# Hymba layer: half of w_out split ahead into DRAM, and the first SSD group's gating moved into the second group

## The chip, the cores and the metric

The kernel runs on one NeuronCore of a Trainium2 chip. The metric is the device time of one execution in microseconds (us). The engines go by the profile's names: PE (TensorE, matmuls), PEld (its weight loads), DVE (VectorE), ACT (ScalarE), POOL (GpSimd) and SP (SyncE, which here only issues DMAs). DMAs are issued on the queues of SP, of POOL and, in the changed kernel, of ACT.

## The reference

One layer over 1024 tokens of width 1024, in float32. All products run on one input projection, whose columns feed a bidirectional state-space branch (SSD, 16 heads in 2 groups, chunks of 128 tokens) and a windowed attention branch (16 heads, 4 KV heads, window 128). Each is gated with SiLU and normed; both go through one output projection.

```python
h = rms_norm(x, norm_in_g)
z, xbc, dt_raw, q, k, v, ga = jnp.split(h @ w_in, PROJ_SPLITS, axis=-1)
xs, Bm, Cm = split(silu(conv5(xbc) + conv_b))            # depthwise, 5 taps
y = ssd(xs, dt_f, ...) + rev(ssd(rev(xs), rev(dt_b), ...)) + d_skip * xs
y_ssd = rms_norm(y * silu(z), ssd_norm_g)                # per group of 512
o = windowed_gqa(q, k, v, rel_bias, sink)                # |i-j| <= 128
y_attn = rms_norm(o * silu(ga), attn_norm_g)
out = x + concat([y_ssd, y_attn]) @ w_out                # w_out: 2048 x 1024
return rms_norm(out, final_norm_g)
```

## The kernel before

Every large product is computed as three PE passes over a high and a low part (hi x hi, hi x lo, lo x hi, type fp32r). So each weight must be split before use: load, an ACT copy that rounds to the high part, and a subtraction that leaves the low part. The input projection runs over 38 weight blocks of 1024 x 128, each loaded once (wraw), split (whi, wlo; the subtraction goes to POOL for every third block, else to DVE) and multiplied with the two halves of the tokens, which stay in SBUF as hhi and hlo.

The stages, by the time of the profile: start (norm, first blocks, the dt and v block), to 58 us; convolutions and backward SSD loop of group 0, to 184; its forward loop, to 297; convolutions of group 1, to 380; its backward loop, to 450; its forward loop, to 540; attention, to about 790; last output products and final norm, to 900. In the SSD stages PE has little SSD work of its own. The function fill(n) puts n halves of projection blocks (24 matmuls of 128 x 512 each) into the loops, and the table FORWARD says how many go where in a forward loop.

In the backward loop, chunks 7 to 0, each chunk's state contribution yo is added to yb_d in DRAM by an accumulating POOL DMA (yb_d already holds the skip term d_skip * xs, written after the convolutions). In the forward loop the chunk's yb starts as the forward state's contribution; an accumulating POOL DMA at line 716 adds yb_d to it in SBUF (chunk 0 is loaded plainly by SP), and at line 723 DVE adds the product y of the scores with the inputs. Then the chunk is gated (lines 726 to 735): zt is loaded, POOL multiplies yb by zt into yg (L729), SP stores yg to y_d, ACT squares (L732), POOL adds the squares in two steps (L733, L735), and after four chunks PE sums them (L605).

w_out's 2048 rows are 16 blocks kb of two pieces of 128 x 512, so 32 "chores". In a chore SP loads a piece (oraw), ACT scales it by the norm's gain (L519) and copies it into hhi (L520), POOL subtracts into hlo (L521): w_out's halves take the place of the projection's hhi and hlo once these are read for the last time. The chores stand between the steps of the attention.

The attention has 32 steps (KV head by query block): logits on PE, a DVE operation with bias and row minimum (L966), the exponential on ACT (L969), transposes on PE (L977), their split on ACT and DVE (L982, L983), products with v. Between them, up to 20 matmuls of projection or output products are fed to PE per step.

The order on each engine is made by a scheduler that lists instructions by a simulated timeline; each engine then works strictly in that order. tc.issue_after(x) keeps an instruction behind x on its queue. A tile of a pool with bufs=1 is one buffer: the next tile of that name waits until every reader of the last one, a DMA too, is done.

Of the kernel before, what the change touches and what calls it, by code (L numbers as in the profile page):

```python
# [10 lines left out]
F32 = mybir.dt.float32  # L11
# [24 lines left out]
def kernel(  # L36
# [21 lines left out]
    def scratch(name, shape, dt):  # L58
        if dbg is not None and name in dbg:
            return dbg[name]  # L60
        return tc.dram_tile(shape, dt, name=name)
# [10 lines left out]
    yb_d = scratch("yb_d", [NG, NSB, P, 512], F32)  # L72
    y_d = scratch("y_d", [NG, NSB, P, 512], F32)
    rd_d = scratch("rd_d", [NKV, 2, 2, 16, 64], F32)
    o_d = scratch("o_d", [NSB, 2, P, 512], F32)

    def pool(stack, name, bufs=1, **kw):
# [182 lines left out]
    def pad_tile():  # L260
# [2 lines left out]
        G.memset(pad[:, S + 2:S + 4], 0.0)  # L263
        return pad

    pads = {}
    square(0)
    root(0)
# [44 lines left out]
    wlo = s1.tile([P, NKB, 288], F32R, tag="wvlo", name="wvlo")  # L313
    wvraw = s1.tile([P, NKB, 288], F32, tag="wvraw", name="wvraw")
    nc.sync.dma_start(out=wvraw, in_=w_vdt)
    ordered(lambda: A.activation(out=whi, in_=wvraw, func=AF.Copy))
    ordered(lambda: G.tensor_tensor(out=wlo, in0=wvraw, in1=whi.bitcast(F32), op=ALU.subtract))
    with tc.issue_after(line["EngineType.Pool"].ins):
        both, dtb, Ab, rb, dsk, msk = small_tables()

    for t, src in zip((snk, dsk), both):
        for a in range(2):
# [177 lines left out]

    def fetch():
        n = split[0] + len(raws)
        if n < len(chores) and len(raws) < RB:
            kb, c = chores[n]
            raw = yp.tile([P, 512], F32, tag="oraw", name="oraw", bufs=RB)
            nc.sync.dma_start(out=raw, in_=w_out[kb * P:(kb + 1) * P, c:c + 512])
            raws.append(raw)

    def chore():
        if split[0] < allowed[0]:  # L510
            if not raws:
                fetch()
            kb, c = chores[split[0]]
            split[0] += 1
            raw = raws.pop(0)
            i, j = divmod(kb % 8, 4)
            hi, lo = (t[i][:, 2 * j:2 * j + 2, :].rearrange("p b e -> p (b e)") for t in (hhi, hlo))
            gain = prm_sb[:, 80 + kb:81 + kb]
            A.activation(out=raw, in_=raw, func=AF.Copy, scale=gain)  # L519
            A.activation(out=hi[:, c:c + 512], in_=raw, func=AF.Copy)  # L520
            G.tensor_tensor(out=lo[:, c:c + 512], in0=raw, in1=hi[:, c:c + 512].bitcast(F32), op=ALU.subtract)  # L521
            wout[kb] = hi, lo
            for _ in range(RB):
                fetch()

    def chores_up_to(n):
        while split[0] < n:
# [69 lines left out]

    sums = []

    def add_sums():  # L600
        ps = bank("t")
        todo = sums[:4]
        del sums[:4]
        for i, (g, c, t) in enumerate(todo):
            T.matmul(ps[:, i:i + 1], lhsT=t, rhs=ones[:, 0:1], start=True, stop=True)  # L605
        g, c, t = todo[0]
        V.tensor_copy(ssq[:, g, c:c + 4], ps[:, 0:4])

    for g in range(NG):
# [4 lines left out]
        for b in range(4):  # L614
            cv = cp.tile([P, S], F32, tag="acc", name="cv")
            th = conv(4 * g + b, cv)
            A.activation(out=th, in_=cv, func=AF.Copy, scale=dsk[:, 4 * g + b:4 * g + b + 1])
            nc.sync.dma_start(out=yb_d[g, :, :, b * P:(b + 1) * P].rearrange("c p l -> p c l"),
                              in_=th.rearrange("p (c l) -> p c l", c=NSB))
            to_tokens(cv, xk[:, :, b * P:(b + 1) * P])  # L620

        if g == NG - 1:
            cpc.close()
# [24 lines left out]
        def y_off(Sx, c, d, dst):  # L648
            et = sp.tile([P, 4, P], F32, tag="et", name="et")
            r = es_d[d, c * NH + g * HPG:c * NH + g * HPG + 1, :]  # L650
            for a in range(2):
                nc.sync.dma_start(out=et[a * 64:(a + 1) * 64].rearrange("p b l -> p (b l)"),
                                  in_=bass.AP(tensor=r.tensor, offset=r.offset + a * 4 * P, ap=[[0, 64], [1, 4 * P]]))
            ps = bank("s")
            for b in range(4):
                T.matmul(ps[:, b * P:(b + 1) * P], lhsT=Sx[:, b * P:(b + 1) * P],  # L656
                         rhs=CT[:, c * P:(c + 1) * P], start=True, stop=True)
            V.tensor_tensor(out=dst, in0=ps, in1=et.rearrange("p b l -> p (b l)"), op=ALU.mult)

        Sb = None  # L660
        for c in range(NSB - 1, -1, -1):
            if Sb is not None:
                yo = sp.tile([P, 512], F32, tag="yo", name="yo", bufs=3)
                y_off(Sb, c, 1, yo)
                G.dma_start(out=yb_d[g, c], in_=yo, accum_op=ALU.add)
            if c > 0:
                Sb = advance(Sb, c, 1)
            if c == 5 and sums:
                add_sums()
            fill(1)  # L670
        Sf = None
# [35 lines left out]
        for c in range(NSB):  # L707
            M = Mn
            if c < NSB - 1:
                Mn = scores(c + 1)  # L710
            yb = sp.tile([P, 512], F32, tag="yo", name="yb", bufs=3)
            if Sf is None:
                nc.sync.dma_start(out=yb, in_=yb_d[g, c])
            else:
                y_off(Sf, c, 0, yb)
                G.dma_start(out=yb, in_=yb_d[g, c], accum_op=ALU.add)
            fill(FORWARD[c][0])
            py = bank("y")
            for h in range(HPG):
                a = h % 2 * 64  # L720
                T.matmul(py[a:a + 64, h // 2 * P:(h // 2 + 1) * P], lhsT=xk[:, c, h * 64:(h + 1) * 64],
                         rhs=M[:, h, :], start=True, stop=True)
            V.tensor_tensor(out=yb, in0=py, in1=yb, op=ALU.add)
            if c < NSB - 1:
                Sf = advance(Sf, c, 0)
            zt = sp.tile([P, 4, P], F32, tag="zt", name="zt", bufs=1)
            nc.sync.dma_start(out=zt, in_=z_d[g * 4:(g + 1) * 4, :, c * P:(c + 1) * P].rearrange("b p s -> p b s"))
            yg = sp.tile([P, 512], F32, tag="yg", name="yg", bufs=1)
            G.tensor_tensor(out=yg, in0=yb, in1=zt.rearrange("p b s -> p (b s)"), op=ALU.mult)  # L729
            nc.sync.dma_start(out=y_d[g, c], in_=yg)  # L730
            y2 = sp.tile([P, 512], F32, tag="y2", name="y2", bufs=1)
            A.activation(out=y2, in_=yg, func=AF.Square)  # L732
            G.tensor_tensor(out=y2[:, 0:256], in0=y2[:, 0:256], in1=y2[:, 256:512], op=ALU.add)  # L733
            sqs = sp.tile([P, P], F32, tag="sqs", name="sqs", bufs=6)
            G.tensor_tensor(out=sqs, in0=y2[:, 0:P], in1=y2[:, P:256], op=ALU.add)  # L735
            sums.append((g, c, sqs))
            if c == 5:
                add_sums()
            if g == NG - 1 and c == 4:
                load_kv(0, 0)  # L740
                load_q(0, 0)
                load_q(0, 1)
            fill(FORWARD[c][1])
# [403 lines left out]
```

## Time and profile before

| | us |
|---|---|
| median of 3 runs | 902.15 (900.38 to 902.24) |
| profiled execution | 901.8 |
| its span | 900.0 |
| PE busy in the span | 850.9 (95%) |
| DVE busy | 574.5 (64%) |
| ACT busy | 488.1 (54%) |
| POOL busy | 366.9 (41%) |

The profile shows one execution. Times count from the span's start; an engine's busy time counts its instructions, not its DMA issues or waits. "Granted clock" is the share of TensorE's full clock that the chip gave it in a stretch. The rows further below come from the same execution; a row's bracket, as [2.41 <-DVE yb L723], says how long the engine had stood idle before that instruction and what ended the wait.

### The profile page before, as it was taken

What the parts mean: (1) busy time and instruction counts of PE and PEld (TensorE: products, weight loads), DVE (VectorE), ACT (ScalarE), POOL (GpSimd) and SP (SyncE); (2) the same over time, 40 slices, a digit from 0 to 9 for tenths busy, and PEclk for the clock granted to TensorE, in tenths of its full rate; (3) what the DMA queues carried; (4) which work ended last, traced back from release to release, by engine and by line L of the source; (5) the groups of instructions that cost most, each with busy time, mean ns of one, the idle gap of its engine ahead of it and who ended that gap; (6) DMA issues with size and microseconds to landing.
All of it is one profiled execution on the core that took longest, in us unless ns stands there. A gap on an engine that the chain in (4) does not pass through costs nothing.

```text
span 900.0 us, 13343 instructions
## 1 busy us (share of the span) xinstructions
PE 850.9 (95%) x4622; PEld 716.0 (80%) x4622; DVE 574.5 (64%) x975; ACT 488.1 (54%) x1112; POOL 366.9 (41%) x331
## 2 busy tenths in 40 slices
PE   6999999998999999999969999999999999799997
PEld 5998788886777888888847787887888888688786
DVE  5675665696897476447769935655766667556433
ACT  5622573464565345524645626788767866765222
POOL 4331012534764201244257551274553741735622
PEclk9999999999999999999998999999999999999999
DMA  9042563675888413577859869879755757424421
GB/s 354 8 114 65 178 192 119 174 220 166 234 233 254 133 47 94 153 189 195 225 145 264 218 182 263 228 197 326 224 152 174 216 132 186 141 59 133 133 87 47
DMA packets 127408, 154.25 MB, mean 171 GB/s; under 512 B 42331, under 2 KB 79899, under 8 KB 127212
## 3 DMA queue, kind: packets, MB, share of 16 engines
q1 hardware_dynamic: 121420, 141.35, 51.7%
q0 software_dynamic: 5776, 11.79, 7.5%
q8 instruction: 36, 0.59, 0.3%
q14 instruction: 32, 0.26, 0.1%
q10 hardware_dynamic: 144, 0.26, 0.1%
HBM read 111.58 MB, written 43.88 MB: 173 GB/s over the span
## 4 chain that ended last, share of the span: by engine, by line
PE 58%; DMA 15%; DVE 10%; issue 7%; POOL 5%; ACT 3%; SPq 1%; POOLq 0%; DVEq 0%; ACTq 0%
PE mm L154 30%; PE mm L781 13%; PE y L999 3%; DMA cb<-cs_d 3%; DMA oraw<-in_w_out_dram 3%; PE s L963 3%; DMA yb<-yb_d 2%; DMA rdb<-rd_d 2%; DMA et<-es_d 2%; PE mm L372 2%; PE t L977 2%; DMA yb_d<-yo 1%; PE s L656 1%; DVE M L702 1%; DMA zt<-z_d 1%
## 5 line engine op out<-in xcount | busy, mean ns | idle before, releaser
L154 PE MATMUL mm<-hlo,whi 128*128 128x512 f32 (+1 forms) x640 | 247.4, 387 | 0.9 <-DVE rs L243 0.5
L154 PE MATMUL mm<-hhi,whi 128*128 128x512 f32 (+1 forms) x640 | 247.9, 387 | 0.0
L154 PE MATMUL mm<-hhi,wlo 128*128 128x512 f32 (+1 forms) x640 | 247.2, 386 | 0.0
L154 PEld LDWEIGHTS mm<-hlo,whi 128*128 128x128 f32 x640 | 121.7, 190 | 24.5 <-issue 1.7
L154 PEld LDWEIGHTS mm<-hhi,wlo 128*128 128x128 f32 x640 | 122.0, 191 | 22.0 <-issue 0.7
L154 PEld LDWEIGHTS mm<-hhi,whi 128*128 128x128 f32 x640 | 122.1, 191 | 21.5 <-issue 0.5
L781 PE MATMUL mm<-hhi,yl 128*128 128x512 f32 (+1 forms) x264 | 104.8, 397 | 0.7 <-POOL yl L773 0.7
L781 PE MATMUL mm<-hhi,yh 128*128 128x512 f32 (+1 forms) x264 | 104.7, 397 | 0.0
L781 PE MATMUL mm<-hlo,yh 128*128 128x512 f32 (+1 forms) x264 | 104.6, 396 | 0.0
L966 DVE CUSTOM_DVE_ANT_0 lg<-s,bias,nsnk 128x320 f32<-128x320 f32 (+2 forms) x128 | 64.5, 521 | 42.3 <-PE s L963 41.4
L969 ACT ACTIVATE lg<-lg,nm 128x320 f32<-128x320 f32 (+2 forms) x128 | 68.5, 535 | 18.5 <-DVE nm L966 16.6
L336 DVE SCALAR_TENSOR_TENSOR acc<-pad,prm_sb,acc 128x1024 f32<-128x1024 f32 x48 | 62.1, 1300 | 23.4 <-ACT acc L333 22.1
L773 POOL TENSOR_TENSOR yl<-y,yh 128x512 fp32r<-128x512 f32 x32 | 41.9, 1309 | 83.8 <-ACT yh L772 59.1
L145 POOL TENSOR_TENSOR wlo<-wraw,whi 128x1024 fp32r<-128x1024 f32 x12 | 30.1, 2509 | 71.0 <-ACT whi L142 71.0
L142 ACT ACTIVATE whi<-wraw 128x1024 fp32r<-128x1024 f32 x36 | 37.9, 1053 | 38.2 <-PE mm L154 34.5
L693 ACT ACTIVATE cb<-cb,ncs 128x128 f32<-128x128 f32 x128 | 39.4, 389 | 30.2 <-DMA cb<-cs_d 30.2
L781 PEld LDWEIGHTS mm<-hhi,yl 128*128 128x128 f32 x264 | 50.2, 190 | 6.9 <-POOL yl L773 1.2
L781 PEld LDWEIGHTS mm<-hhi,yh 128*128 128x128 f32 x264 | 50.3, 190 | 5.7
L781 PEld LDWEIGHTS mm<-hlo,yh 128*128 128x128 f32 x264 | 50.1, 190 | 5.5
L983 DVE TENSOR_TENSOR pl<-t,ph 128x512 fp32r<-128x512 f32 (+1 forms) x64 | 40.6, 654 | 21.4 <-ACT ph L982 20.7
L521 POOL TENSOR_TENSOR hlo<-oraw,hhi 128x512 fp32r<-128x512 f32 x32 | 41.0, 1289 | 26.5 <-ACT hhi L520 26.2
L145 DVE TENSOR_TENSOR wlo<-wraw,whi 128x1024 fp32r<-128x1024 f32 x24 | 34.3, 1428 | 22.2 <-ACT whi L142 19.6
(236 smaller groups left out, 1772.3 us busy)
## 6 DMA issues: line engine op xcount, KB each, us to landing
wraw<-in_w_blk_dram SPq DMA_DIRECT2D x38, 512.0 KB, 4.7
cb<-cs_d SPq DMA_DIRECT2D x32, 512.0 KB, 5.8
qt<-q_d SPq DMA_DIRECT2D x32, 256.0 KB, 4.0
oraw<-in_w_out_dram SPq DMA_DIRECT2D x32, 256.0 KB, 4.2
et<-es_d SPq DMA_DIRECT2D x56, 128.0 KB, 4.9
yb_d<-pad SPq DMA_DIRECT2D x8, 512.0 KB, 4.0
z_d<-gz SPq DMA_DIRECT2D x16, 256.0 KB, 3.5
zt<-z_d SPq DMA_DIRECT2D x16, 256.0 KB, 3.7
```

What stands on the lines that cost most here:

```text
L142: A.activation(out=hi, in_=raw, func=AF.Copy)
L145: eng.tensor_tensor(out=lo, in0=raw, in1=hi.bitcast(F32), op=ALU.subtract)
L154: yield T.matmul(ps, lhsT=l[:, kb, :], rhs=r[sh][:, kb, cols], start=(n == 0), stop=(n == 3 * NKB - 1))
L336: V.scalar_tensor_tensor(out=acc, in0=pad[:, k:k + S], scalar=cw[:, blk * 6 + k:blk * 6 + k + 1], in1=acc, op0=ALU.mult, op1=ALU.add)
L521: G.tensor_tensor(out=lo[:, c:c + 512], in0=raw, in1=hi[:, c:c + 512].bitcast(F32), op=ALU.subtract)
L693: A.activation(out=E[:, h, :], in_=E[:, h, :], func=AF.Identity, bias=ncs[:, 0, c, hh:hh + 1])
L773: G.tensor_tensor(out=lo, in0=t, in1=hi.bitcast(F32), op=ALU.subtract)
L781: yield T.matmul(ps[:, cols], lhsT=l[:, j * P:(j + 1) * P], rhs=r[:, dh * 512 + cols.start:dh * 512 + cols.stop], start=first and n == 0, ...
L963: pe(lambda: T.matmul(ps[:, 0:c1 - c0], lhsT=self.qt[:, sub, 2 * hp:2 * hp + 2, :], rhs=kt[:, k0:k0 + c1 - c0], start=(i == 0), stop=(i == ...
L966: V.tensor_tensor_reduce(out=l, in0=ps[:, d0 - c0:d1 - c0], in1=bias[:, hp, d0 - f0:d1 - f0], scale=-1.0, scalar=nsnk[:, sk], op0=ALU.add, ...
L969: A.activation(out=l, in_=l, func=AF.Exp, scale=-1.0, bias=nm, accum_out=sm)
L983: V.tensor_tensor(out=pl[0:w, 0:n], in0=ps[0:w, 0:n], in1=ph[0:w, 0:n].bitcast(F32), op=ALU.subtract)
```

## The change

Three edits stand in it.

1. At the start, the small tables (dt bias, A, rb, d_skip, mask: six DMAs on POOL's queue) are issued before the first norm and not behind the dt and v block's last split, and that block's split (128 x 2304) is cut into two ACT and four POOL pieces.
2. The second half of w_out's rows (kb 8 to 15, 16 pieces) is split during group 1 by split_ahead: SP loads a piece into wr, ACT scales it and copies the high part into wh, an ACT DMA writes wh to wo_d, POOL subtracts in place and a POOL DMA writes wr to wo_d. Two pieces are tied behind each of the four skip writes of the convolutions, and one behind the loads of each chunk of the backward loop. wr and wh have one buffer each. In the attention, these chores are then two plain loads of 256 KB each from wo_d.
3. Group 0's forward loop no longer reads yb_d and gates: yb (for chunk 0 an ACT copy of y) is accumulated into yb_d by a POOL DMA after the addition. The gating, now gate_y, is done with four chunks in group 1's convolutions and four in its backward loop (c = 7 to 4), from yb_d. Group 1 gates in its forward loop as before.

```diff
+    wo_d = scratch("wo_d", [2, 8, P, D], F32)
...
+    both, dtb, Ab, rb, dsk, msk = small_tables()
     pads = {}
     square(0)
...
-    ordered(lambda: A.activation(out=whi, in_=wvraw, func=AF.Copy))
-    ordered(lambda: G.tensor_tensor(out=wlo, in0=wvraw, in1=whi.bitcast(F32), op=ALU.subtract))
-    with tc.issue_after(line["EngineType.Pool"].ins):
-        both, dtb, Ab, rb, dsk, msk = small_tables()
+    for k in (slice(0, 4), slice(4, 8)):
+        ordered(lambda: A.activation(out=whi[:, k], in_=wvraw[:, k], func=AF.Copy))
+    for n in range(0, NKB, 2):
+        k = slice(n, n + 2)
+        ordered(lambda: G.tensor_tensor(out=wlo[:, k], in0=wvraw[:, k], in1=whi[:, k].bitcast(F32), op=ALU.subtract))
...
-        if n < len(chores) and len(raws) < RB:
+        if n < 16 and len(raws) < RB:
...
+            if kb >= 8:
+                for n, t in enumerate((hi, lo)):
+                    nc.sync.dma_start(out=t[:, c:c + 512].bitcast(F32), in_=wo_d[n, kb - 8, :, c:c + 512])
+                wout[kb] = hi, lo
+                return
...
+    def split_ahead(n, behind):
+        kb, c = chores[16 + n]
+        raw = sp.tile([P, 512], F32, tag="wr", name="wr", bufs=1)
+        hi = sp.tile([P, 512], F32R, tag="wh", name="wh", bufs=1)
+        with tc.issue_after(behind.ins):
+            nc.sync.dma_start(out=raw, in_=w_out[kb * P:(kb + 1) * P, c:c + 512])
+        A.activation(out=raw, in_=raw, func=AF.Copy, scale=prm_sb[:, 80 + kb:81 + kb])
+        A.activation(out=hi, in_=raw, func=AF.Copy)
+        nc.scalar.dma_start(out=wo_d[0, kb - 8, :, c:c + 512], in_=hi.bitcast(F32))
+        G.tensor_tensor(out=raw, in0=raw, in1=hi.bitcast(F32), op=ALU.subtract)
+        nc.gpsimd.dma_start(out=wo_d[1, kb - 8, :, c:c + 512], in_=raw)
...
+    def gate_y(g, c, behind, yb=None):
+        zt = sp.tile([P, 4, P], F32, tag="zt", name="zt", bufs=1)
+        yg = sp.tile([P, 512], F32, tag="yg", name="yg", bufs=1)
+        y2 = sp.tile([P, 512], F32, tag="y2", name="y2", bufs=1)
+        with ExitStack() as st:
+            if behind is not None:
+                st.enter_context(tc.issue_after(behind.ins))
+            if yb is None:
+                nc.sync.dma_start(out=yg, in_=yb_d[g, c])
+            nc.sync.dma_start(out=zt, in_=z_d[g * 4:(g + 1) * 4, :, c * P:(c + 1) * P].rearrange("b p s -> p b s"))
+        G.tensor_tensor(out=yg, in0=yg if yb is None else yb, in1=zt.rearrange("p b s -> p (b s)"), op=ALU.mult)
...
-            nc.sync.dma_start(out=yb_d[g, :, :, b * P:(b + 1) * P].rearrange("c p l -> p c l"),
+            skip = nc.sync.dma_start(out=yb_d[g, :, :, b * P:(b + 1) * P].rearrange("c p l -> p c l"),
                               in_=th.rearrange("p (c l) -> p c l", c=NSB))
             to_tokens(cv, xk[:, :, b * P:(b + 1) * P])
+            if g == NG - 1:
+                split_ahead(2 * b, skip)
+                split_ahead(2 * b + 1, skip)
+            if g > 0:
+                gate_y(g - 1, b, skip)
...
-                y_off(Sb, c, 1, yo)
+                skip = y_off(Sb, c, 1, yo)
                 G.dma_start(out=yb_d[g, c], in_=yo, accum_op=ALU.add)
             if c > 0:
                 Sb = advance(Sb, c, 1)
-            if c == 5 and sums:
+            if g == NG - 1:
+                split_ahead(15 - c, skip)
+            if g > 0 and c >= 4:
+                gate_y(g - 1, 11 - c, skip)
+            if g > 0 and c in (5, 1):
                 add_sums()
...
-            if Sf is None:
-                nc.sync.dma_start(out=yb, in_=yb_d[g, c])
-            else:
+            if Sf is not None:
                 y_off(Sf, c, 0, yb)
-                G.dma_start(out=yb, in_=yb_d[g, c], accum_op=ALU.add)
+            if g == NG - 1:
+                if Sf is None:
+                    nc.sync.dma_start(out=yb, in_=yb_d[g, c])
+                else:
+                    G.dma_start(out=yb, in_=yb_d[g, c], accum_op=ALU.add)
...
-            V.tensor_tensor(out=yb, in0=py, in1=yb, op=ALU.add)
+            if Sf is None and g < NG - 1:
+                A.activation(out=yb, in_=py, func=AF.Copy)
+            else:
+                V.tensor_tensor(out=yb, in0=py, in1=yb, op=ALU.add)
+            if g < NG - 1:
+                G.dma_start(out=yb_d[g, c], in_=yb, accum_op=ALU.add)
...
+            if g == NG - 1:
+                gate_y(g, c, None, yb)
+                if c == 5:
+                    add_sums()
```

The line numbers of the kernel after that the rows below use: split_ahead is L541 (load), L542 and L543 (ACT), L544 (ACT's DMA), L545 (POOL), L546 (POOL's DMA); gate_y is L632 to L638; the accumulating store is L781; the exponential is L1018, the split of w_in's blocks L141 to L147.

POOL in the first forward loop, before (S the state, xd the weighted input, yb the chunk's output, yg, y and sqs the gating):

```order
L643 TENSOR_TENSOR S_1937<-S_1796,dec 128x512
L628 TENSOR_TENSOR xd<-xk,wst 128x512
L716 DMA yb<-yb_d 128x512
L729 TENSOR_TENSOR yg<-yb,zt 128x512
L643 TENSOR_TENSOR S_2043<-S_1937,dec 128x512
L628 TENSOR_TENSOR xd<-xk,wst 128x512
L733 TENSOR_TENSOR y_1803<-y_1803 128x256
L735 TENSOR_TENSOR sqs<-y_1803 128x128
```

and after:

```order
L689 TENSOR_TENSOR S_1932<-S_1801,dec 128x512
L674 TENSOR_TENSOR xd<-xk,wst 128x512
L781 DMA yb_d<-yb 128x512 x2
L689 TENSOR_TENSOR S_2028<-S_1932,dec 128x512
L674 TENSOR_TENSOR xd<-xk,wst 128x512
L689 TENSOR_TENSOR S_2160<-S_2028,dec 128x512
L781 DMA yb_d<-yb 128x512
```

The read of yb_d and the gating are gone from between the state updates; in their place stands the accumulating store of yb, with nothing of the loop behind it.

ACT where the SSD ends and the attention begins, before (y is the last gating's square, gth and qhi finish projection halves, lg is the exponential):

```order
L732 ACTIVATE y_4736<-yg 128x512
L142 ACTIVATE whi<-wraw 128x1024
L452 ACTIVATE gth<-mm 128x512
L462 ACTIVATE qhi<-mm 128x512
L969 ACTIVATE lg_4839,sm<-lg_4839,nm 128x192
L969 ACTIVATE lg_4839,sm<-lg_4839,nm 128x256
```

and after, up to the second of the last three splits (the last one, the same three rows, follows, and then the exponential, L1018, with 128x192 first):

```order
L635 ACTIVATE y_4874<-yg 128x512
L144 ACTIVATE whi<-wraw 128x1024
L456 ACTIVATE gth<-mm 128x512
L542 ACTIVATE wr<-wr,prm_sb 128x512
L543 ACTIVATE wh<-wr 128x512
L544 DMA wo_d<-wh 128x512
L466 ACTIVATE qhi<-mm 128x512
L542 ACTIVATE wr<-wr,prm_sb 128x512
L543 ACTIVATE wh<-wr 128x512
L544 DMA wo_d<-wh 128x512
L542 ACTIVATE wr<-wr,prm_sb 128x512
L543 ACTIVATE wh<-wr 128x512
```

Of the four last splits one stands ahead of qhi and three between qhi and the first exponential.

SP at the same place, before (acc is the residual for the output products, vz, khh and kll are v and k tiles):

```order
L730 DMA y_d<-yg 128x512
L761 DMA acc<-in_x_dram 128x512 x2
L455 DMA ga_d<-gz 128x512
L938 DMA vz_4831<-v_d 64x5x128
L938 DMA vz_4832<-v_d 64x5x128
L581 DMA khh<-k_d 64x640 x2
L581 DMA kll<-k_d 64x640
L477 DMA q_d<-qhi 64x8x64 x2
L477 DMA q_d<-qlo 64x8x64 x2
```

and after:

```order
L634 DMA y_d<-yg 128x512
L541 DMA wr<-in_w_out_dram 128x512
L810 DMA acc<-in_x_dram 128x512 x2
L459 DMA ga_d<-gz 128x512
L481 DMA q_d<-qhi 64x8x64 x2
L481 DMA q_d<-qlo 64x8x64 x2
L541 DMA wr<-in_w_out_dram 128x512 x3
L987 DMA vz_4972<-v_d 64x5x128
L987 DMA vz_4973<-v_d 64x5x128
L603 DMA khh<-k_d 64x640 x2
```

The load of the thirteenth split stands behind the last store of y_d, and those of the last three behind the stores of q; the v and k loads stand behind them.

## Rows read from the trace of the kernel before

**Rows 1.** Stretches: start:end, length, busy of PE, PEld, DVE, ACT, POOL, clock, DMA, GB/s.

```profile
184.00:297.00 113.00, 103.96 (x562) 84.03 (x561) 89.56 (x98) 64.36 (x156) 60.40 (x49) 0.95 0.75 220
297.00:380.00 83.00, 83.00 (x388) 69.11 (x387) 48.38 (x41) 39.34 (x50) 9.27 (x14) 1.00 0.36 98
450.00:540.00 90.00, 79.13 (x442) 63.23 (x441) 64.81 (x75) 42.16 (x101) 56.05 (x48) 0.96 0.74 202
540.00:772.00 232.00, 226.63 (x1316) 192.21 (x1315) 149.73 (x408) 169.13 (x442) 105.14 (x81) 1.00 0.72 205
772.00:800.00 28.00, 23.02 (x120) 19.69 (x119) 13.43 (x39) 21.13 (x55) 16.45 (x15) 0.88 0.38 123
```

**Rows 2.** Timeline of the start: start us, duration us, engine, line, operation, [idle before].

```profile
7.41 0.55 POOL L244 TENSOR_TENSOR rs<-rs,nhalf 128x1 f32<-128x1 f32 x1 [0.93 <-DVE rs L243]
...
38.94 5.16 POOL L317 TENSOR_TENSOR wvlo<-wvraw,wvhi 128x2304 fp32r<-128x2304 f32 x1 [7.89 <-ACT wvhi L316]
...
40.92 4.27 DVE L145 TENSOR_TENSOR wlo<-wraw,whi 128x1024 fp32r<-128x1024 f32 x1 [3.37 <-ACT whi L142]
...
47.24 1.54 POOL L324 COPY snk<-sink 64x8 f32<-64x8 f32 x2 [0.24 <-DMA sink<-in_sink_dram]
```

**Rows 3.** Waits of PE, 0 to 75: total us, times, longest us.

```profile
PE mm L372 <- DVE vt L379: 1.8, 1, 1.8
```

**Rows 4.** Waits of DVE, 184 to 300.

```profile
DVE yb L723 <- DMA yb<-yb_d: 14.8, 5, 5.1
DVE cb L694 <- DMA cb<-cs_d: 5.2, 4, 2.1
```

**Rows 5.** Timeline of DVE and POOL in the first forward loop.

```profile
185.14 1.21 DVE L694 TENSOR_TENSOR cb<-cb,ncs 128x1024 f32<-128x1024 f32 x1
...
202.32 2.39 POOL L145 TENSOR_TENSOR wlo<-wraw,whi 128x1024 fp32r<-128x1024 f32 x1
...
203.33 2.46 DVE L694 TENSOR_TENSOR cb<-cb,ncs 128x1024 f32<-128x1024 f32 x1 [2.11 <-DMA cb<-cs_d]
...
219.37 0.69 DVE L723 TENSOR_TENSOR yb<-y,yb 128x512 f32<-128x512 f32 x1 [5.10 <-DMA yb<-yb_d]
```

**Rows 6.** POOL's groups by line, 184 to 297: count, busy us, mean ns, idle before.

```profile
L729 POOL TENSOR_TENSOR yg<-yb,zt 128x512 f32<-128x512 f32 x8 | 13.0, 1626 | 25.3 <-DVE yb L723 18.4 <-DMA q_d<-qhi 5.3 <-DMA zt<-z_d 1.4
...
L733 POOL TENSOR_TENSOR y<-y 128x256 f32<-128x256 f32 x8 | 10.8, 1350 | 1.7 <-ACT y L732 1.7
...
L716 POOL DMA_DIRECT2D yb<-yb_d x7 | 6.2, 887 | 4.7 <-DVE yb L658 2.0 <-DMA et<-es_d 2.0 <-DVE ssq L607 0.8
L735 POOL TENSOR_TENSOR sqs<-y 128x128 f32<-128x128 f32 x7 | 5.8, 831 | 0.3
```

**Rows 7.** The tile oraw: durations in ns, min/median/max, and its loads.

```profile
L519 ACT ACTIVATE oraw<-oraw,prm_sb x32: 707/723/727, 557.2 to 789.5; 128x512 f32<-128x512 f32 x32
L520 ACT ACTIVATE hhi<-oraw x32: 612/624/636, 582.5 to 790.3; 128x512 fp32r<-128x512 f32 x32
L521 POOL TENSOR_TENSOR hlo<-oraw,hhi x32: 1267/1288/1312, 583.2 to 791.0; 128x512 fp32r<-128x512 f32 x32
...
DMA to landing us min/median/max: 2.5/4.2/6.9
```

**Rows 8.** DMA issues: queue, count, KB each, median us to landing.

```profile
yb_d<-yo POOLq DMA_DIRECT2D x14, 256.0 KB, 5.3
...
rd_d<-rdt POOLq DMA_DIRECT2D x8, 8.0 KB, 3.1
```

**Rows 9.** Timeline where the attention begins.

```profile
539.44 2.94 POOL L117 TENSOR_TENSOR rs_s<-rs_s,nhalf 128x16 f32<-128x16 f32 x1
...
541.48 0.46 ACT L969 ACTIVATE lg<-lg,nm 128x192 f32<-128x192 f32 x1
```

**Rows 10.** Waits of ACT, 540 to 800.

```profile
ACT oraw L519 <- DMA oraw<-in_w_out_dram: 15.8, 15, 2.7
```

**Rows 11.** DVE's taps in the convolutions, 297 to 380.

```profile
L336 DVE SCALAR_TENSOR_TENSOR acc<-pad,prm_sb,acc 128x1024 f32<-128x1024 f32 x24 | 31.3, 1304 | 15.6 <-ACT acc L333 14.8
```

## What the change was predicted to do

> **What bounds the kernel now.** I read the page first: PE is busy for nearly the whole span, and no other engine comes near it. So a change pays only where PE stands still, and it costs wherever it makes PE stand still. Next I cut the span into stages [rows 1], where the reader is to see how PE's busy time stands to the length of the stretch. PE fills the second group's convolutions to the last microsecond (83.00 of 83). It lacks 113 − 103.96 = 9.0 us in the first forward loop, 10.9 in the second, 5.4 over the attention and 5.0 in the 28 us where the attention ends. Three of these stretches also show a granted clock below full: 0.95, 0.96 and 0.88. Third came the waits of VectorE and ScalarE, which name who made PE late, and last the timeline around the places that the change moves.
>
> The profiled execution took 901.8 us (span 900.0). The median of the runs is 902.15, so the two differ by less than the runs scatter, and the sum below stands on 901.8.
>
> **The start: −1 us (−3 to +2).** GpSimd's subtraction of the dt and v block is one instruction of 5.16 us, and the VectorE split that began beside it took 4.27 us and ended 1.1 us after it [rows 2], as if it had begun only then. In four pieces VectorE may get in between. PE's wait at the end of this chain is 1.8 us [rows 3], so no more than that, and a little of what hangs on it, is to be had. Against it, the small tables now stand early on GpSimd's queue, and copies such as the pair of 1.54 us come between the first powers that the start waits for, the second at 7.41 [rows 2]. If all of that lands on the path it costs about 2. I take −1.
>
> **The first forward loop: −9 us (−14 to −2).** VectorE's addition into yb waits 14.8 us in five places for the accumulating read of yb_d, the longest 5.1 [rows 4], and the row at 219.37 is that longest one [rows 5]. In the new code nothing waits for this read: yb is added first and then accumulated into DRAM. PE's idle time is 9.0 us and the clock of 0.95 loses 5.6 more over 113 us, so 14.7 is the ceiling. What is late next are the cb loads (5.2 us in four places [rows 4]). I charge these in full: 14.7 − 5.2 = 9.5, taken as −9. The low end of the gain, −2, is the case in which PE's other inputs, scores and states, end the same gaps. GpSimd sheds 8 × (1.63 + 1.35 + 0.83) = 30 us here [rows 6], which is cover, since it was idle for half of the stretch.
>
> **Convolutions and backward loop of the second group: +1 (−1 to +7).** Eight gatings and ahead of them splits arrive here. PE is full and its work is unchanged; VectorE has 34.6 us free and GpSimd 73.7 [rows 1], and they hide the new work. The upper end is worked out under rival B.
>
> **The second forward loop: +2 (−3 to +11).** Five of the sixteen splits fall here by the order. Each costs GpSimd a subtraction of 1.29 [rows 7] and a DMA issue of about 0.9 (the mean of seven such issues is 887 ns [rows 6]), 11 us in all on an engine that has 34 free, but it stands between state updates. All of it on the path is the upper end. The lower end is the 3.6 us that the clock of 0.96 loses. I take a fifth of 11.
>
> **The end of the SSD: +30 (+24 to +37).** This term decides. In the order after, three complete splits stand on ScalarE between the last qhi and the first exponential of the attention, and a fourth before that qhi; before, the exponential followed qhi at once. ScalarE works in order. There is one buffer wr, so split n+1 can't load before split n's remainder has been written to DRAM from it. One turn of that ring is load, scaling, copy, subtraction, write. The first four are the old chore's own: 4.2 + 0.72 + 0.62 + 1.29 = 6.83 [rows 7]. The write is a plain one of 256 KB on GpSimd's queue, which the trace doesn't have. Its nearest rows on that queue are the 8 KB write, 3.1, and the accumulating write of 256 KB, 5.3 [rows 8]. I take 3.1, since the DMA engines have little else to do while everyone waits; the turn is then 9.9, say 10. With the shortest load, 2.5, and 3.1 it is 8.2; with 4.2 and 5.3 it is 12.1.
>
> By the Trainium skill (DMA: Bandwidth & Descriptors, "Anatomy of one DMA — SWDGE (gpsimd) path") such a write costs 2.0 us fixed and its bytes at 436 GB/s, an estimate of 2.6 us; the turn would be 9.4 and this term about 1 us smaller. No run here shows a plain write of this size on that queue.
>
> The ring's start: the write of the thirteenth split stands behind the power on GpSimd that ends at 539.44 + 2.94 = 542.4 [rows 9], and lands 3 us later, at about 545 (544 to 547.7). Then two whole turns, the last load and the last two ScalarE steps: 545 + 2 × 10 + 4.2 + 1.3 = 570.5. The first exponential stood at 541.48 [rows 9], so it is 29 us later. Nothing covers that. Behind the waiting ScalarE instruction are all exponentials; for these wait the probability transposes on PE, and PE has only some ten matmuls of the last projection and the first logits before them. Behind the waiting SP load stand the v, k and bias loads, which come late by as much and no more. The restart at the lower of PE's two clock levels, as in the stretch with 0.88, adds about 1. The ends: 544 + 16.4 + 3.8 = 564.2 gives +23, and 547.7 + 24.2 + 5.5 = 577.4 gives +36, each with 1 for the clock.
>
> **The attention: −6 (−11 to +5).** Sixteen of 32 chores lose two ScalarE steps and one on GpSimd: 16 × 1.34 = 21.5 us and 16 × 1.29 = 20.6. ScalarE's 15.8 us of waiting for oraw in 15 places [rows 10] should halve. PE's loss is 5.4 + 5.0 idle and 0.12 × 28 = 3.4 by the clock, 13.8 in all [rows 1]; ScalarE is busy for 75% of the last of these stretches, and the second half of the chores stands there. I take −6, somewhat less than half, since most gaps in this stage end on softmax steps that stay. The high side: 32 plain loads, in two bursts of 4.2 MB, go on SP ahead of the y and q loads. At the stage's 205 GB/s a burst lasts 20 us beside the rest; if that outlasts the buffers by a few microseconds it costs about 5.
>
> Sum: 901.8 − 1 − 9 + 1 + 2 + 30 − 6 = 918.8, so 919.
>
> **Rivals.**
> A, faster: the gains come and the ring costs little, because the last splits run earlier in time than their place in the order suggests, or the loads and writes are far quicker than the rows. The gains alone give 901.8 − 13 = 889. The point from which it decides is a ring that delays the exponential by less than 12 us, so that two turns take under 4, or 2 each. For it speaks only that the small DMAs meet idle queues. Against it, the three computing steps alone are 2.63 a turn [rows 7] and the shortest load 2.5. Chance 0.10.
>
> B, slower still: VectorE and GpSimd hold each other up in the second group. The row at 203.33 shows a VectorE addition of 2.46 us that began inside GpSimd's 2.39; the same line alone takes 1.21 [rows 5]. It ended 1.08 after GpSimd's did, as if it had waited whole. At the start the pair of 5.16 and 4.27 reads the same way [rows 2]. In the convolutions four blocks get 2 × 1.29 + 3.81 = 6.4 us of GpSimd each, 25.6 in all. If VectorE waits for all of it beside its 48.4 busy and its 15.6 of waiting for ScalarE in the taps [rows 11], the stage needs 89.6 of 83: +6.6. In the second forward loop 5 × 1.29 add 6.5. In place of my +3 that is +13: 929. Against it, overlap by chance hits only part. Chance 0.10.
> The Trainium skill (SBUF — State Buffer, "Who interferes with whom") says that an operation of VectorE with two inputs in SBUF contends with GpSimd's reads through a shared port; by that rule B would be the rule and not chance. The two pairs agree with it.
>
> D, near balance: the delay at its low end and both gains near their ceilings: 901.8 − 3 − 14 + 3 + 24 − 11 = 901. Chance 0.06.
>
> **How the numbers follow.** Forecast 0.74, A 0.10, B 0.10, D 0.06. About 0.2% is what the runs can tell from no change. Slower by more than that: forecast and B, 0.84. D gives 0.04 to the same and 0.02 to faster; with A faster has 0.12. Adding the half widths of the six terms as independent gives about ±14, or 905 to 933; with D, and a part of B, the range is 900 to 935.
>
> **What would show it.** Right: a PE gap of 25 to 33 us between the last projection and the first transposes, ended by ScalarE's exponential, with three splits back to back, 9 to 12 us apart; no wait of the yb addition for yb_d in the first forward loop, and PE's idle time there under 4 us. Wrong: split turns under 5 us, or exponentials ahead of them; a PE gap in the convolutions (B); y or q loads ending PE waits in the attention.

## The result and the profile after

The changed kernel takes 926.50 us (median of 4 runs, 925.75 to 927.02) against 901.26 beside it: ratio 1.0287, 95% interval 1.0264 to 1.0309. The prediction was 919 with a range of 900 to 935. The profiled span grew from 900.0 to 924.5, that is +24.5, where the sum had +17.

Stretches of the kernel after, columns as in [rows 1] (length, busy time and count of PE, PEld, DVE, ACT and POOL, clock, DMA share, GB/s):

```profile
184.00:297.00 113.00, 111.86 (x610) 90.35 (x609) 89.49 (x102) 63.83 (x154) 35.76 (x28) 1.00 0.74 201
297.00:380.00 83.00, 81.88 (x385) 67.85 (x383) 48.77 (x40) 44.26 (x60) 29.72 (x33) 1.00 0.51 159
380.00:450.00 70.00, 60.58 (x303) 49.19 (x301) 52.69 (x52) 32.07 (x73) 46.41 (x42) 0.98 0.98 281
450.00:540.00 90.00, 83.35 (x465) 67.36 (x465) 67.00 (x80) 51.61 (x117) 58.50 (x51) 0.98 0.87 250
540.00:572.00 32.00, 8.45 (x25) 6.56 (x26) 3.44 (x13) 8.54 (x22) 12.49 (x13) 0.58 0.48 152
572.00:800.00 228.00, 219.37 (x1269) 186.31 (x1269) 146.66 (x394) 154.26 (x408) 91.62 (x72) 0.99 0.72 205
```

Two rows stand out against [rows 1]. In the first forward loop PE is idle for 1.1 us where it was for 9.0, at a full clock. Between 540 and 572 PE works for 8.45 of 32 us, at a mean clock of 0.58, nearer to the lower of its two levels (1.2 GHz) than to the upper. The row of 380 to 450 is the third to see; before, the same stretch read:

```profile
380.00:450.00 70.00, 70.00 (x355) 58.31 (x354) 44.63 (x57) 30.66 (x72) 26.86 (x24) 1.00 0.78 206
```

The DMA engines go there from 0.78 to 0.98 busy, and PE, which was full, loses 9.4 us. Who made it wait, from the waits of PE in 380 to 450 of the kernel after (total us, times, longest; before there were none):

```profile
PE s L684 <- DVE xl L678: 2.5, 3, 2.0
PE t L646 <- POOL sqs L638: 1.9, 2, 1.0
PE s L684 <- ACT xh L677: 1.7, 1, 1.7
PE s L702 <- DVE S L690: 1.6, 1, 1.6
```

These are the inputs of the state updates (L684), a state itself (L702) and the sums of the gating that was moved here (L646). Whether the busy DMA engines are behind it stays open: e8 below has them at 0.97 in the same stretch and PE busy for 65.69 of 70.

Now the end of the SSD. ScalarE's timeline after, from the last qhi ahead of the attention to the first exponential (L1018), which stood at 541.48 before [rows 9]:

```profile
540.79 0.60 ACT L466 ACTIVATE qhi<-mm 128x512 fp32r<-128x512 f32 x1 [0.46 <-ACT wh L543]
549.55 0.72 ACT L542 ACTIVATE wr<-wr,prm_sb 128x512 f32<-128x512 f32 x1 [8.17 <-DMA wr<-in_w_out_dram]
...
557.63 0.72 ACT L542 ACTIVATE wr<-wr,prm_sb 128x512 f32<-128x512 f32 x1 [6.70 <-DMA wr<-in_w_out_dram]
...
565.90 0.72 ACT L542 ACTIVATE wr<-wr,prm_sb 128x512 f32<-128x512 f32 x1 [6.89 <-DMA wr<-in_w_out_dram]
...
567.77 0.46 ACT L1018 ACTIVATE lg<-lg,nm 128x192 f32<-128x192 f32 x1 [0.49 <-ACT wh L543]
```

The three last splits are 8.1 and 8.3 us apart, each waits for its load, and the exponential follows the third. The loads in turn waited on SP for the writes from wr (SP's waits in 536 to 580), and VectorE had written what the first exponential reads long before, from 542.03 on:

```profile
SPq L541 <- DMA wo_d<-wr: 21.1, 4, 7.7
```

```profile
542.03 0.41 DVE L1015 CUSTOM_DVE_ANT_0 lg<-s,bias,nsnk 128x192 f32<-128x192 f32 x1
```

So for some 25 us the exponential waited for nothing but its place on ScalarE. PE's timeline at the same place:

```profile
542.50 0.58 PE L1012 MATMUL s<-khh,qt 128*128 128x256 f32 x1 [3.75 <-DVE nm L1015]
...
543.09 0.63 PE L156 MATMUL mm<-hlo,whi 128*128 128x512 f32 x1
...
568.37 0.48 PE L1026 MATMUL t<-ident,lg 128*128 128x128 f32 x1 [20.60 <-ACT lg L1018]
...
570.00 0.63 PE L156 MATMUL mm<-hhi,whi 128*128 128x512 f32 x1
...
572.99 0.39 PE L156 MATMUL mm<-hhi,wlo 128*128 128x512 f32 x1
```

A gap of 20.6 us, ended by the exponential; and matmuls of 0.63 us after the wait of 3.75 and after the long one, 0.39 again from 572. The wait of 3.75 belongs to the ring too: it was for the first logits' minimum (nm), which VectorE made behind the low part of q, and this waited for qhi, which stood behind the thirteenth split on ScalarE (the first row above).

**Where the 24.5 us are.** Since nearly every matmul exists in both kernels, the n-th matmul of a line (lines 154, 781 and 999 of before: projection, output and value products) can be set against the n-th of that line in the other trace; the median of these shifts within 3 us of a time of before says how far the kernel is ahead or behind there. Read at 180, 296, 534 and 580 us of before and at the end, the differences of successive readings give, in us:

```
                       to 180   forward g0   group 1   end of SSD   attention on   sum
forecast                 -1        -9          +3         +30           -6         +17
the change              +1.1     -12.1        +4.2       +36.4         -5.1       +24.5
e1 twelve ahead         +0.1     -11.8        +5.6        +2.9         -6.7        -9.9
e2 splits only          +0.1      -0.7        +3.6       +20.2         -6.3       +16.9
e3 gating only          -0.2     -12.4        +9.4        -1.9         +1.3        -3.8
e4 start only           -0.4      -1.3        +1.2        +1.8         +1.3        +2.6
e5 two more turns       +1.2     -11.2        +8.2       +48.1         -3.6       +42.7
e6 eight ahead          -0.2     -11.9        +7.9        -0.8         -2.1        -7.1
e7 gating in conv.      -0.2     -12.9       +11.7        -2.0         -1.8        -5.2
e8 both                  0.0     -12.5        +5.5        +1.6         -6.5       -11.9
e9 no arithmetic        +0.4     -11.9        +6.6        -1.1         -1.0        -7.0
e10 no gating           +1.9      -9.9        -2.8        -1.8         -1.3       -13.9
e11 splits in group 0   +9.8      +1.4        +6.0        -1.5         -4.0       +11.7
```

Here "to 180" holds the start and the first group up to its forward loop, and group 1 is the second group (its convolutions and both loops). Row e4, whose code differs only at the start, shows what a single profile can say: up to 2 us per stage are no finding.

### The profile page after: what moved, and what is told of

Same layout as the page of the kernel before. It is cut to its first block, busy times and chain, and to the rows that moved or that the text cites. A ratio compares the mean times of both kernels' runs of the same rounds, so it can differ in the third digit from the quotient of the medians.

```text
span 924.5 us, 13491 instructions
## 1 busy us (share of the span) xinstructions
PE 852.0 (92%) x4622; PEld 715.2 (77%) x4622; DVE 583.8 (63%) x974; ACT 491.1 (53%) x1114; POOL 373.4 (40%) x351
## 4 chain that ended last, share of the span: by engine, by line
PE 43%; DMA 17%; DVE 11%; POOL 11%; issue 10%; ACT 6%; SPq 2%; POOLq 0%; ACTq 0%; DVEq 0%
PE mm L156 20%; PE mm L830 12%; DMA zt<-z_d 3%; PE y L1048 3%; POOL yg L633 2%; DMA cb<-cs_d 2%; PE s L1012 2%; PE mm L376 2%; PE t L1026 2%; DMA et<-es_d 1%; DMA rdb<-rd_d 1%; DMA yg<-yb_d 1%; DMA oraw<-in_w_out_dram 1%; DVE M L754 1%; DMA xk<-in_x_dram 1%
## 5 line engine op out<-in xcount | busy, mean ns | idle before, releaser
L1018 ACT ACTIVATE lg<-lg,nm 128x320 f32<-128x320 f32 (+2 forms) x128 | 68.6, 536 | 29.0 <-DVE nm L1015 26.3
L340 DVE SCALAR_TENSOR_TENSOR acc<-pad,prm_sb,acc 128x1024 f32<-128x1024 f32 x48 | 65.3, 1363 | 27.9 <-ACT acc L337 26.6
L1026 PE MATMUL t<-ident,lg 128*128 128x128 f32 x240 | 37.7, 277 | 22.6 <-ACT lg L1018 21.1
L1026 PEld LDWEIGHTS t<-ident,lg 128*128 128x128 f32 x240 | 30.6, 142 | 32.3 <-ACT lg L1018 22.3
L147 POOL TENSOR_TENSOR wlo<-wraw,whi 128x1024 fp32r<-128x1024 f32 x12 | 29.8, 2487 | 63.4 <-ACT whi L144 63.4
L144 ACT ACTIVATE whi<-wraw 128x1024 fp32r<-128x1024 f32 x36 | 37.9, 1052 | 28.8 <-PE mm L156 26.3
```

What stands on the lines that cost most here:

```text
L144: A.activation(out=hi, in_=raw, func=AF.Copy)
L147: eng.tensor_tensor(out=lo, in0=raw, in1=hi.bitcast(F32), op=ALU.subtract)
L340: V.scalar_tensor_tensor(out=acc, in0=pad[:, k:k + S], scalar=cw[:, blk * 6 + k:blk * 6 + k + 1], in1=acc, op0=ALU.mult, op1=ALU.add)
L1018: A.activation(out=l, in_=l, func=AF.Exp, scale=-1.0, bias=nm, accum_out=sm)
L1026: pe(lambda: T.transpose(ps[0:g[1] - g[0], j * 256 + hp * P:j * 256 + (hp + 1) * P], self.lg[:, hp, g[0]:g[1]], ident))
```

## The experiments

The theory is the ring: splits in one buffer, in order on ScalarE, ahead of the first exponential. The rival is that the traffic added to the second group and the late v, k and bias loads cost the time. That the loads are late comes from the same ring, so no run has one without the other; what tells them apart is the row of 542.03 above, by which the first exponential's input was there.

**e1: no split at the end.** Twelve pieces ahead; the last four stay chores.

```diff
-            if g == NG - 1:
+            if g == NG - 1 and c >= 4:
                 split_ahead(15 - c, skip)
```

(the chores of the last four pieces load and split as before)

> Only 12 pieces are split ahead (the last four, tied to chunks 3 to 0 of the backward loop, are chores in the attention as before). No split then stands on ScalarE between the last qhi and the first exponential. Theory (the one-buffer ring ahead of the first exponential costs 36 us of PE): the 20.6 us gap is gone, the second group ends some 7 us earlier than before and the attention gives back about 4 of its 5: about 891 us, ratio 0.985 to 0.992. Rival (the added DMA traffic in the second group and the late v and k loads cost the time): 12 splits and their traffic are still there, so 910 or more.

Measured 893.36 us, ratio 0.9926 (0.990 to 0.9952). The theory's number was 891. PE's waits between 380 and 580:

```profile
PE s L685 <- DVE xl L679: 6.7, 4, 3.6
PE t L647 <- POOL sqs L639: 3.7, 3, 1.9
PE s L703 <- DVE S L691: 2.6, 1, 2.6
PE y L775 <- DVE yb L780: 1.3, 2, 0.9
```

No wait for the exponential is left; the end of the SSD costs 2.9 instead of 36.4, with twelve of sixteen splits and their traffic still there. That decides against the traffic as the main cause. (The v, k and bias loads are on time here, so e1 says nothing of these.) It also turns the change into a gain, of 0.7%.

**e2: the splits alone.** The gating is back in the first forward loop, as in the kernel before.

> The splits ahead with the start edit, the first group gated in its own forward loop as before. Theory (ring): no gain in the first forward loop, the ring at the end as in the change: 928 to 934. Rival (traffic in the second group): without the gating's loads and stores the second group's DMAs fall, so 905 to 915.

Measured 919.61, ratio 1.0218 (1.0185 to 1.0251): neither. PE's wait and ScalarE's splits:

```profile
PE t L1014 <- ACT lg L1006: 12.6, 2, 12.2
```

```profile
538.86 0.72 ACT L542 ACTIVATE wr<-wr,prm_sb 128x512 f32<-128x512 f32 x1 [0.67 <-DMA wr<-in_w_out_dram]
...
549.93 0.72 ACT L542 ACTIVATE wr<-wr,prm_sb 128x512 f32<-128x512 f32 x1 [6.33 <-DMA wr<-in_w_out_dram]
558.16 0.72 ACT L542 ACTIVATE wr<-wr,prm_sb 128x512 f32<-128x512 f32 x1 [6.84 <-DMA wr<-in_w_out_dram]
559.94 0.45 ACT L1006 ACTIVATE lg<-lg,nm 128x192 f32<-128x192 f32 x1 [0.40 <-ACT wh L543]
```

My number for the theory was wrong in its count: in this kernel's order only two splits stand behind the last qhi, not three. The exponential comes 7.8 us earlier than in the change, about a turn. PE arrives at the end 9.8 us later than in the change (+3.0 against -6.8), and its gap is 12.2 instead of 20.6. So the ring's end does not follow PE: with PE later and one turn fewer it comes earlier by about a turn.

**e5: two more turns.** The last two pieces are split and written once more, behind the sixteen.

```diff
                 split_ahead(15 - c, skip)
+                if c == 0:
+                    split_ahead(14, skip)
+                    split_ahead(15, skip)
```

> The change with the last two pieces split and written a second time, behind the sixteen: five splits then stand on ScalarE between the last qhi and the first exponential, where the change has three and the kernel with the splits only has two. Theory (the gap is turns of the one-buffer ring at 8.1 to 8.3 us): PE's gap grows from 20.6 to about 37 us and the time by 16 to 17: 942 to 944. Rival (the gap is set by what else is late there, the v, k and bias loads or the restart): 927 to 932.

Measured 944.52, ratio 1.0476 (1.0431 to 1.052). PE's wait:

```profile
PE t L1029 <- ACT lg L1021: 37.6, 2, 37.1
```

With 0, 2, 3 and 5 splits behind the last qhi (e1, e2, the change, e5) the gap is none, 12.2, 20.6 and 37.1: 8.2 to 8.4 for each split beyond the second, as the turns on ScalarE are apart. The rival's 927 to 932 is out. All these runs keep one buffer; the same splits with two were not run.

**e3: the gating alone.** No splits ahead; all chores as before.

> The start edit and the moved gating, no splits ahead: all 32 chores in the attention as before. Theory (the gating gains in the first forward loop and costs little later): +1 at the start, -12 in the first forward loop, 0 to +4 in the second group: 891 to 895. Rival (the gating's DMAs and VectorE-GpSimd collisions in the second group make up for it): 900 or more.

Measured 896.47, ratio 0.9955 (0.993 to 0.998). That lies between the theory and the rival: the first forward loop gives its 12.4 us, but the second group takes 9.4 back.

**e4: the start alone.**

> The start edit alone (small tables early, dt and v split in pieces). Theory: the second power of GpSimd comes later and PE starts about 2 us later, of which the shorter dt and v split gives back 1 to 2: 902 to 904, that is +1. Rival (the pieces gain as forecast): -1.

Measured 901.30 against 900.38, ratio 1.0009 (0.9984 to 1.0035): nothing that can be told from no change, though the number fits the theory.

**e6: eight ahead**, all tied to the convolutions.

> Eight pieces split ahead, all tied to the convolutions, none to the backward loop; the other eight of the second half are chores in the attention. Theory (no split ahead of the exponential; four splits less among the second group's state updates give 1 to 2 us there, four more chores cost the attention 1.5 to 2): 892 to 895, level with twelve ahead. Rival (each split in the SSD costs as its DMA traffic): 889 or less.

Measured 894.68, ratio 0.9915 (0.9884 to 0.9945), as the theory has it: level with e1. The attention gives 2.1 instead of 6.7, and this alone doesn't tell whether the count of splits matters.

**e7: the gating in the convolutions.** Two of the first group's chunks at each block, none in the backward loop, no splits.

```diff
-                gate_y(g - 1, b, skip)
+                gate_y(g - 1, 2 * b, skip)
+                gate_y(g - 1, 2 * b + 1, skip)
```

> No splits ahead; the first group's eight gatings all tied to the second group's convolutions, two to each block, none to the backward loop. The kernel with the gating moved lost 9.4 us between the convolutions' end and the attention. Theory (what it lost is GpSimd's gating standing among the state updates): half or more of the 9.4 comes back: 888 to 892. Rival (VectorE and GpSimd collide, which then stretches the convolutions, or the DMA traffic of the gating is the price wherever it stands): 896 or more, with PE waiting before 380.

Measured 896.83, ratio 0.9953 (0.9936 to 0.9969): the theory that the place among the state updates is what costs falls. The second group takes back 11.7 us. The rival's time is met but hardly its sign: PE waits for only 1.2 us between 297 and 380, and the rest of the loss comes later.

**e8: e1 and e7 together.**

> Twelve pieces ahead, with all eight gatings tied to the convolutions. Theory: twelve ahead measured 893.4, and the gating out of the backward loop gives 3 to 5: 888 to 891. Rival (the convolutions can't hold both; splits and gatings spill into the backward loop as one chain): 893 or more.

Measured 890.89, ratio 0.9879 (0.9843 to 0.9914), the fastest of the versions that compute everything, ahead of both kernels. Its interval overlaps e1's at the edge, so how much the place of the gating adds isn't settled.

**e9 and e10: what takes the gating's gain back.** e9 leaves out the first group's gating arithmetic and keeps its transfers. e10 leaves out its loads as well and stores yb plainly to y_d in the first forward loop. Both outputs lack that gating.

> The gating moved and no splits ahead, with the first group's gating arithmetic left out: its loads and its store of y_d stay tied where they are, but the multiplication, the square and the two additions are missing (GpSimd writes ones in place of the sums). Theory (GpSimd's and ScalarE's gating work between the state updates takes back the 9 to 12 us): 886 to 890. Rivals: the loads and stores take it back, or the second group's loops can't use an earlier start whatever stands in them; with either 894 to 898.

> As e9, with the loads left out too: the first group is not gated at all, and yb is stored plainly to y_d in its own forward loop; the second group's convolutions and loops hold nothing of it but the ones. If the DMA traffic takes the gain back: 886 to 890 here, against 894 to 898 in e9. If the second group's loops can't use an earlier start: 894 to 898 here too. If the arithmetic does: as e9.

Measured 891.23 and 888.11, ratios 0.9915 (0.9886 to 0.9944) and 0.9869 (0.9839 to 0.9899). So e9 falls between its two forecasts, and e10 meets 886 to 890. Without any of it, the second group keeps the earlier start and even adds 2.8; so its loops can use it. From e3 to e10, the gating and its transfers together cost about 8 us (0.9955 - 0.9869 of 900), and these intervals don't touch. How it divides is open: by the runs the arithmetic and the loads take about 4 each, by the second group in the single profiles 2.8 and 9.4, and e9's interval overlaps both others.

**e11: the splits in the first group.** Twelve there (convolutions and backward loop), four in the second group's convolutions.

> All sixteen pieces split ahead, but twelve in the first group (eight tied to its convolutions, four to the first chunks of its backward loop) and four in the second group's convolutions; the gating as in the change. No split stands near the first exponential. Theory: the attention gives its 5 to 6 us as in the change, the first group's convolutions have room for the splits (PE full, GpSimd 25 of 126 us busy), the second group loses what it lost with the gating alone or less: 888 to 891. Rival (the splits slow the first group's convolutions or its forward loop): 895 or more.

Measured 909.62, ratio 1.0116 (1.0072 to 1.016): the rival. There was room on GpSimd, but ScalarE waits there for the ring's loads, in 58 to 200:

```profile
ACT wr L542 <- DMA wr<-in_w_out_dram: 31.7, 6, 10.8
```

PE's waits in the same stretch, of which there were none before, are led by ScalarE:

```profile
PE s L686 <- ACT xh L679: 3.7, 2, 2.0
```

I read it as the same mechanism in another place: a split whose load must wait for the last split's write holds everything behind it on ScalarE. No run sets it apart from the traffic there. 9.8 us were lost by 180, the first forward loop gives nothing (+1.4, where the change has -12.1; why isn't shown), and the attention's gain, 4.0, is not enough.

## Why the prediction was right, and where it was off

**What decides: right.** The forecast named the ring ahead of the first exponential as the term that outweighs the rest, slower by 17 us against 25 measured. e1 takes it away and the kernel is 7 us faster than before; e5 adds two turns and pays for two (18 us more than the change, 16.5 of them in the gap). Two of the signs that I had named missed their numbers all the same: the gap is 20.6 us and not 25 to 33, and the splits are 8.1 to 8.3 us apart and not 9 to 12.

**The size of that term, +30 against +36.4, is where most of the miss is, and the step that failed is the one from the ring's end to the loss.** The turn itself was put too long, 10 us against 8.1 to 8.3. Its parts, from the DMA issues between 546.5 and 567 in the kernel after (queue, count, KB, us to landing):

```profile
wr<-in_w_out_dram SPq DMA_DIRECT2D x3, 256.0 KB, 2.6
...
wo_d<-wr POOLq DMA_DIRECT2D x2, 256.0 KB, 2.3
```

I had 4.2 and 3.1. The load's median from a busy stage [rows 7] was too long for one in which nothing else runs; its minimum of 2.5 was the right row. For the write, the estimate of 2.6 from the Trainium skill (DMA: Bandwidth & Descriptors, "Anatomy of one DMA — SWDGE (gpsimd) path") was nearer than my row; the run shows 2.3. The ring started 2 us later than I put it. GpSimd's power, ahead of the thirteenth write, stood behind the thirteenth subtraction and ended at 544.56, not at 542.4; the write came behind it, and SP could issue the fourteenth load only when that had landed:

```profile
541.63 2.93 POOL L119 TENSOR_TENSOR rs_s<-rs_s,nhalf 128x16 f32<-128x16 f32 x1
544.53 0.62 POOL L546 DMA_DIRECT2D wo_d<-wr  x1
```

```profile
546.97 16.36 SPq L541 DMA_DIRECT2D wr<-in_w_out_dram  x3
```

So the exponential came at 567.77 where I had 570.5, 26.3 us later than before and not 29. Yet the stage lost more. I took the delay from 541.48, where the exponential stood before, and then also counted the gains ahead of it. But the ring's end does not move with PE; PE was 6.8 us early at 534 and only waited longer. The gain of the first forward loop, less what the second group took, could not be had together with this delay. 26.3 + 6.8 = 33.1. The restart, which I had put at 1, adds nothing to that: read at 547 to 555 of before, behind the first exponentials, the shift is +25.9. From there to 564 it grows to +29.6, and these 3.7 us are a late step of the softmax (L1031):

```profile
585.85 0.47 PE L1048 MATMUL y<-ph,vt 128*128 128x256 f32 x1 [3.00 <-ACT ph L1031]
```

```profile
581.03 0.72 ACT L528 ACTIVATE oraw<-oraw,prm_sb 128x512 f32<-128x512 f32 x1 [3.71 <-DMA oraw<-in_w_out_dram]
```

The step stands on ScalarE behind three w_out pieces, the first of which waited for its load; before, it stood ahead of them (at 553.42, the first piece at 557.23). This is the order's doing, and no term of my sum had it. e2 has the same wait (3.8 us), e5 has not.

**First forward loop, -9 against -12.1: right, a little low.** DVE's waits in 184 to 300, which answer to [rows 4]:

```profile
DVE acc L340 <- ACT acc L337: 10.8, 1, 10.8
DVE cb L745 <- DMA cb<-cs_d: 5.6, 5, 2.3
```

(The first row is the convolutions of group 1, which now begin inside this window.) The wait for yb_d is gone. The cb waits are still there, as foreseen, but they no longer reach PE, and I had charged them in full.

**The second group, +3 against +4.2: the sum right by luck, the reasoning not.** I wrote that VectorE's and GpSimd's free time would hide the moved work behind a full PE, and read that free time from the convolutions alone. In the backward loop PE is not full any more, 60.58 of 70, with the DMA engines at 0.98; part of it is regained in the forward loop, where PE had stood before. e3 and e10 show that the gating with its transfers costs some 8 us; my working had no term for the transfers.

**Start, -1 against +1.1: within its bounds, not within what a run can tell (e4).** PE's first matmul, after and before:

```profile
9.22 0.48 PE L260 MATMUL mm<-ident,xt 128*128 128x128 f32 x1 [9.22 <-DVE rs L245]
```

```profile
7.33 0.47 PE L258 MATMUL mm<-ident,xt 128*128 128x128 f32 x1 [7.33 <-DVE rs L243]
```

It stands 1.9 later, and not by the path that I had named. The first power ends at 6.35, no later than before (6.49); VectorE's scaling of the tokens, which PE's first matmul needs, stood behind a step that waited for the load of prm_sb:

```profile
8.30 0.20 DVE L276 TENSOR_SCALAR prm_sb<-prm_sb 128x72 f32<-128x72 f32 x1 [2.66 <-DMA prm_sb<-in_prm_dram]
```

This load landed 6.6 us after its issue, where before it took 4.2, with five of the tables' six DMAs issued beside it; VectorE waits here in every run with the start edit (1.3 to 3.5 us) and did not before. The copies on GpSimd hold only the second power, by 0.35 us. The shift is 2.9 by 35 us and 1.1 from 72 on; I put the 1.8 that came back down to the dt and v block in pieces, which no run has alone. VectorE's split that began beside that block took 2.36 against 4.27 [rows 2]:

```profile
43.81 2.36 DVE L147 TENSOR_TENSOR wlo<-wraw,whi 128x1024 fp32r<-128x1024 f32 x1 [3.37 <-ACT whi L144]
```

**Attention, -6 against -5.1: right.** ScalarE's wait for oraw, which I expected to halve, in 572 to 830, answering to [rows 10]:

```profile
ACT oraw L528 <- DMA oraw<-in_w_out_dram: 9.9, 7, 3.7
```

Seven places instead of fifteen, 9.9 us instead of 15.8.

**The rivals.** A is out: nothing runs ahead of its place in the order, and a turn is 8 us, not 2. B is out: the convolutions with eight splits and four gatings leave PE at 81.88 of 83, with VectorE's busy time at 48.77 where it was 48.38 [rows 1], and the second group costs 4.2 where B had 13. D is out, its delay being above 24.

## What to carry to other kernels

Work put "ahead" into a slack stage goes where the order lets it, and with one buffer and a write in the ring it runs at the ring's latency, not at its engine's: sixteen times 1.35 us of ScalarE became three waits of 6.7 to 8.2 us in front of the stage that was to profit. Count the instructions that stand between the last work of one stage and the first of the next on each in-order engine, and multiply by the turn.

A delay that comes from a chain with its own clock is an absolute time. What is saved ahead of it is waited away again, so such gains are not summed with it.

## What the runs showed of the hardware that I had not expected

A plain write of 256 KB on GpSimd's queue lands in 2.3 us when nothing else moves, and a load of the same size in 2.6, against 4.2 in the median of the busy attention [rows 7]. A load of 48 KB (prm_sb) landed in 6.6 us instead of 4.2 with five small tables' DMAs issued beside it on GpSimd's queue.

After the wait of 3.75 us that ended at 542.50 the granted clock is 0.50 up to 547.8, the lower of the two levels, and the matmuls of 512 columns took 0.63 us. After the long gap it is 0.50 from 568.3 to 572 and 0.98 from 572 to 582, where most of them took 0.39 again.
